# Other places for gate groups, weight loads, query rests and MoBA values in a hybrid attention layer on one Trainium2 core

## The chip, the cores and the metric

The kernel runs on one core of a Trainium2 chip. The core has TensorE (PE, with its weight loads shown as PEld), VectorE (DVE), ScalarE (ACT), GpSimd (POOL) and SyncE (SP), which here issues nearly all DMAs. The metric is the device time of one execution in microseconds. Three executions of the kernel before gave 666.95, 663.0 and 665.05 us, a median of 665.05.

## The reference

One layer is computed for a prompt of 512 tokens and for 8 samples with one new token and 1024 cached positions each; both share all weights. Two token mixers run on the same modulated input, are projected up, merged by sigmoid gates, projected out and normalized. Cut to what matters:

```python
shift, scale, gate = jnp.split(jax.nn.silu(c) @ w_ada + b_ada, 3, axis=-1)
h = x * (1.0 + scale[:, None, :]) + shift[:, None, :]
parts = jnp.split(h @ w_in, np.cumsum(IN_WIDTHS)[:-1], axis=-1)
(a_q, a_kc, a_vc, a_ks, a_vs, a_kw, a_vw, a_g, a_z, b_q, b_k, b_v, b_z, m_a, m_b) = parts
...
o_a = nsa_attention(...)    # compressed blocks + selected blocks + window, gated per head
o_b = moba_attention(...)   # top-3 past blocks by q . mean(k), and the own block
y_a = (o_a.reshape(bsz, t, NSA_WIDTH) * jax.nn.silu(a_z)) @ w_up_a
y_b = (o_b.reshape(bsz, t, MOBA_WIDTH) * jax.nn.silu(b_z)) @ w_up_b
mixed = (jax.nn.sigmoid(m_a) * y_a + jax.nn.sigmoid(m_b) * y_b) @ w_out
x_new = layer_norm(DEEPNORM_ALPHA * x + gate[:, None, :] * mixed, ln_g, ln_b)
```

The cached keys and values of the samples come from paged pools in HBM. The third part of `w_ada`, which gives `gate`, is 1024 x 1024.

## The kernel before

**Columns of work.** The kernel multiplies the 520 columns of tokens (512 + 8) by blocks of 128 weight columns. One such block is a *dense*: 48 matmuls in the order of instructions (24 for each half of the tokens), with the tokens and the weights each split into a high and a low fp32r part (hTh, hTl; hl holds both parts of a weight). Names of denses: q and z (queries and gate path of the sparse mixer), bq, bk, bv, bz (MoBA), ma and mb (the two merge gates; "m6" is ma6 and mb6). The table FILLS says which denses fill which stage. The result of a merge gate that is ready before the last stage is written to `m_d` in HBM and read again later.

**Stages.** 0 to 57 us: the modulation, with its weights ada_ss. 57 to 160: the compression network on cached pages (`phis`), merged with FILLS[0]. 160 to 177: compressed branch. 177 to about 491: eight `attend(pi)`, one for each pair of heads of the prompt, each merged with a part of the samples' attention (`dec`, from cached pages) and with the denses of FILLS[1..8]. About 491 to 549: the denses of FILLS[9], the gate groups g0 to g3 and the rest of `dec`. From 549: `up`, out projection, norm.

**What sets the order.** A `Flow` wraps a generator that yields its costs; `merge` always steps the flow with the smallest share done, so the yields, DEC_SHARE, DEC, DEC_PACE, PHIS and ATT set the order of PE's instructions. From the first pair to the end of FILLS[9], `behind` chains PE's instructions and `queue` chains SP's loads in the order in which the code issues them; SP's queue holds a load until its buffer is free, and all that stands behind it waits too. At most eight of SP's DMAs are under way.

**Weights.** W is a feed with four raw buffers (NRAW; tile raw, 128x1024, 0.52 MB) and three split buffers (hl). `use` (L320) serves a dense and asks for weights two ahead; `take` serves a gate group with raw tiles of ada_g and asks up to three ahead. ACT writes the high part (L305), DVE or GpSimd the low part (L226). A gate group (gen_gate, tile s) is eight matmuls of 512 columns in the trace.

**Pages.** The samples' pages come through C with two buffers (CRAW): slck (selected keys), wink, mobk, slcv (selected values, gathered by an indirect DMA that GpSimd issues), winv, and mobv, the MoBA values, sixteen blocks of four loads of 0.26 MB.

**Inside a pair.** `prepare` splits the queries of a pair into high parts (ACT) and rests, for head groups g = 0 and 1: DVE makes the rest in q2 (L1000), GpSimd that in qx (L1002). `probs` ends with GpSimd's scaling of p (L1051), which the transposes in `turn` (L191, pt) read.

Of the kernel before, what the change touches and what calls it, by code (L numbers as in the profile page):

```python
# [18 lines left out]
T = 512  # L19
# [18 lines left out]
         ["m2", "m3"],  # L38
         ["z0", "bv1", "m4"],
         ["z1", "m5"],  # L40
         ["bk1", "bv2", "z2"],
         ["bk2", "bv3", "bk3"],
         ["z3", "bz0"],
         ["bz1", "m6"],
         ["bz2", "g0", "g1", "bz3", "g2", "g3", "m7"]]
CMP_FILLS = ["bq3", "bk0", "bv0"]
DEC_SHARE = [0.1, 0.236, 0.375, 0.51, 0.575, 0.63, 0.765, 0.89]
DEC, DEC_PACE = 58800.0, 0.9
PHIS = 49353.58399999998
ATT = [16000] * 4 + [8000] * 3 + [10400]  # L50
SECOND = [3, 4, 6, 7]
LIM = 0, 384, 384, 768
# [6 lines left out]
LO_ENG = "dp", "pd", "dp"  # L59

SEQ = (COLS[:3]
       + [n for f in (FILLS[0], CMP_FILLS, *FILLS[1:]) for i in f if i != "ks" for n in ([f"ma{i[1]}", f"mb{i[1]}"] if i[0] == "m" else
                                          [f"g{2 * int(i[1])}", f"g{2 * int(i[1]) + 1}"] if i[0] == "g" else [i])]
       + [n for c in range(8) for n in [f"up{c}"] + ([f"wo{c // 2 - 1}"] if c % 2 and c > 1 else [])]
       + ["wo3"])
# [64 lines left out]
def f32(ap):  # L130
    return ap.bitcast(F32)
# [32 lines left out]
def build(tc, A):  # L164
    nc = tc.nc
# [52 lines left out]
    D = {}  # L218
# [12 lines left out]
    with ExitStack() as es:  # L231
# [35 lines left out]
        class Feed:  # L267
# [49 lines left out]

            def use(self):
                u = self.used = self.used + 1
                self.load_to(self.units[u][0] + 2)  # L320
                self.split_to(u + 1)
                return self.part.pop(u)

# [246 lines left out]
        DENSE = 16 * 333  # L570
# [79 lines left out]
        TM = {}  # L650
# [8 lines left out]
                return pair(tag, dtype)  # L659
            return D["fm"].tile([128, 2, NT], dtype, name="m", tag="m", bufs=7)  # L660

        def gen_m(c):

            if "fm" in D:
                t = TM[c] = m_tile(F32, TM_TAGS[c])
            for i, n in enumerate(("ma", "mb")):
                acc = yield from dense(f"{n}{c}")
                to = t[:, i] if "fm" in D else D["at"].tile([128, NT], F32, name="mg", bufs=2)
                for bk in range(2):
                    nc.scalar.activation(to[:, HALF[bk]], acc[bk][:, :HB], AF.Tanh, scale=0.5)  # L670
                if "fm" not in D:
                    post(lambda to=to, i=i: ld(m_d[c][:, i], to))
                    D["put"] = c + 1
# [16 lines left out]
                nc.scalar.copy(D["ga"][hf], p)  # L690

        def fill_cost(names):
            return max(1.0, sum(2 * DENSE if n[0] == "m" else 1000 if n[0] == "g" else 1700 if n == "ag" else 1 if n == "ks" else DENSE for n in names))

        def fills(names):
            for n in names:
                k = int(n[-1]) if n[-1].isdigit() else 0
                if n == "ks":
                    yield from gen_k(n, ksn[:, 0, :], first["ks"])
                elif n == "kw":  # L700
                    yield from gen_k(n, ksn[:, 1, :])
                elif n in ("vs", "vw"):
                    yield from gen_v(n, 0 if n == "vs" else 1)
                elif n == "ag":
                    yield from gen_gates()
                elif n[0] == "q":
                    yield from gen_q(n, k)
                elif n[0] == "m":
                    yield from gen_m(k)
                elif n[0] == "g":  # L710
                    yield from gen_gate(k)
                elif n[0] == "z":
                    yield from gen_z(n, k)
                elif n[:2] == "bq":
                    yield from gen_q(n, 4 + k)
                elif n[:2] == "bz":
                    yield from gen_z(n, 4 + k)
                elif n[:2] == "bv":
                    yield from gen_v(n, 2 + k)
                else:  # L720
                    yield from gen_k(n, ksm[:, k, :])
# [72 lines left out]
        def phi_prompt(kc, vc):  # L794
            ut = []
            for kv, ev in enumerate((kc, vc)):
                u = u_tile()
                ut.append(u[:, :, 0:528].rearrange("p x (l n) -> p x l n", l=8))
                with tc.issue_after(D["act"].ins), tc.issue_after(D["dve"].ins):
                    nc.scalar.copy(ut[kv][:, 0, :, 64:66], pos[:, kv])  # L800
                    nc.vector.tensor_sub(ut[kv][:, 1, :, 64:66], pos[:, kv], f32(ut[kv][:, 0, :, 64:66]))
                eh = pp.tile([128, 2, 512], F32R, name="eh", tag="craw", bufs=2)
                nc.scalar.copy(eh[:, 0], ev[:, :T])
                lo(eh[:, 1], ev[:, :T], eh[:, 0])
                for x, cp in enumerate((nc.scalar.copy, nc.vector.tensor_copy)):
                    v = f32(eh[:, x]).rearrange("p (u l s) -> p l u s", l=8, s=2)
                    for g in range(2):
                        for l2 in range(2):
                            cp(ut[kv][OWN[l2], x, :, g * 32:g * 32 + 32], v[OWN[g], :, :, l2])
            yield 3000  # L810
            gl = yield from units(64, lambda kv, x, l: ut[kv][:, x, l, :])
            p = p_pt()
            for j, (wa, x) in enumerate(((w2h, 0), (w2l, 0), (w2h, 1))):
                mm(p[:, 0:64], wa[:, 0:128], gl[:, x, :64], j == 0, j == 2)
            for j, (x, wa) in enumerate(((0, w2h), (0, w2l), (1, w2h))):
                mm(p[:64, 64:128], gl[:, x, :64], wa[:, 128:192], j == 0, j == 2)
            yield 600
            x2 = pp.tile([128, 64], F32, name="x2")
            nc.scalar.activation(x2, p[:, 0:64], AF.Identity, scale=0.5, bias=phib[:, 1:2])
            nc.scalar.copy(ck2[:, 0, :], x2)  # L820
            lo(ck2[:, 1, :], x2, ck2[:, 0, :], "d")
            for g in range(2):
                rows = slice(g * 32, g * 32 + 32)
                nc.vector.scalar_tensor_tensor(cv2[rows, g], p[rows, 64:128], 0.5, b2v[rows], op0=OP.mult, op1=OP.add)
# [12 lines left out]
        def phi_pair(bp):  # L837

            us = [u_tile().rearrange("p x (k q u) -> p x q k u", k=16, q=16) for _ in range(2)]
            for ch in range(4):  # L840
                load_chunks(bp * 4 + ch + 1)
                raw = craw.pop(bp * 4 + ch)
                for kv in range(2):
# [1 line left out]
                    dh, dl = (us[kv][:, x, ch * 4:ch * 4 + 4] for x in range(2))  # L845
                    nc.scalar.copy(dh, src)  # L846
                    lo(dl, src, dh)
                yield 0
            uv = [u.rearrange("p x q k u -> p x (k q u)") for u in us]
            gl = yield from units(256, lambda kv, x, l: uv[kv][:, x, l * 256:l * 256 + 256])  # L850
            p = p_pt()
# [133 lines left out]
        def prepare(pi):  # L985
# [8 lines left out]
            for g in range(2):  # L994
                own, oth = OWN[g], OWN[1 - g]

                q2 = at.tile([128, T], F32R, name="q2", bufs=3)
                qx = at.tile([128, T], F32R, name="qx", bufs=3)
                nc.scalar.copy(q2[own], y[own, pi, :T])  # L999
                nc.vector.tensor_sub(q2[oth], y[own, pi, :T], f32(q2[own]))  # L1000
                nc.scalar.copy(qx[oth], y[own, pi, :T])
                nc.gpsimd.tensor_sub(qx[own], y[own, pi, :T], f32(q2[own]))  # L1002
                Q2[pi, g] = q2, qx

        GRP = [[(0, 0), (0, 1), (0, 2), (0, 3)], [(1, 1), (1, 2), (1, 3), (3, 3)], [(2, 2), (2, 3)]]
# [204 lines left out]
        def new_p(d):  # L1210
# [2 lines left out]
            tr(p[:8, :128], d, ident)  # L1213
            t = de.tile([8, 128], F32, name="np", bufs=2)
            nc.vector.tensor_copy(t, p[:8, :128])
            yield 600
            return t

        def own_p(x, col, name):
# [4 lines left out]
        def dec_a():  # L1224
# [23 lines left out]
                yield from C.fetch(0 if q else 1000)  # L1248
            nc.vector.tensor_add(xw[:, :512], xw[:, :512], s)
            nc.vector.tensor_copy(xw[:, 512:513], snew[:, 1:2])  # L1250
            nc.vector.tensor_add(xs[:, 896:1024], xs[:, 896:1024], bdn[:, 0:128])
            late = nc.vector.tensor_copy(xs[:, 1024:1025], snew[:, 0:1])
            xv = xs[:, 64:960].rearrange("p (j c) -> p j c", j=14)
            nc.vector.tensor_add(xv, xv, dn[:, :14, None].to_broadcast([128, 14, 64]))
            softmax(xs, 1025, gd[:, 1:2], de)
# [50 lines left out]
        def dec_b():  # L1306
# [8 lines left out]

            xo = D["xo"]
            nc.vector.tensor_mul(xo, xo, mask("maskn").rearrange("p (a c) -> p a c", a=3))
            yield 500
            total()
            yield 700  # L1320
            p = p_e()
            for i in range(3):
                mm(p[:, :32], xo[:, i], const("seln"), i == 0, i == 2)
# [10 lines left out]
            nc.vector.tensor_add(xv, xv, dm[:, :4, None].to_broadcast([128, 4, 256]))  # L1334
            softmax(xm, 1025, ones, de)
            dm2 = own_p(xm, 1024, "onem")
            yield 1500
            tpm = yield from turn_p([xm[:, k * 128:k * 128 + 128] for k in range(8)], True)
            nm = yield from new_p(dm2)
            p = p_e()  # L1340
# [1 line left out]
                mm(p[grp(t), :128], nm[:, grp(t)], vnew[:, 2 + t], True, True)  # L1342
            xn = de.tile([128, 128], F32, name="xn")
            nc.vector.tensor_mul(xn, p[:, :128], mask("maskh"))
            yield 300
            om = {}
            for q in range(2):
                o = p_e()
# [5 lines left out]
                    yield from C.fetch(1000)  # L1354
                x = om[q] = de.tile([128, 512], F32, name="xo2", tag="x" if q else "xw")
                nc.vector.tensor_mul(x, o, mask("maskm"))
            yield 300
            p = D["ym"] = p_e()
            mm(p[:, :32], xn, const("selx"), True, False)
            for q in range(2):  # L1360
# [16 lines left out]
                yield fa.done - d  # L1377

        done = 0.0
        for pi in range(8):  # L1380
            fl = Flow(fills(FILLS[pi + 1]), fill_cost(FILLS[pi + 1]))
            if pi == 0:

                for _ in range(8):
                    fl.step()
                fl.total, fl.done = fl.total - fl.done, 0.0
            merge(Flow(attend(pi), ATT[pi]), Flow(part(DEC_SHARE[pi]), max(1.0, (DEC_SHARE[pi] - done) * DEC)), fl)
            done = DEC_SHARE[pi]
        while posts:
            posts.pop(0)()  # L1390
# [5 lines left out]
        ga = D["ga"] = [fm.tile([128, 512], F32, name="ga", bufs=2) for _ in range(2)]  # L1396
        for c in range(D.get("put", 0)):
            TM[c] = m_tile(F32, TM_TAGS[c])
            ld(TM[c], m_d[c])
        merge(Flow(fills(FILLS[9]), fill_cost(FILLS[9])), Flow(part(2.0), max(1.0, (1 - done) * DEC / DEC_PACE)))  # L1400
        while posts:
            posts.pop(0)()
        behind[0] = queue[0] = False
# [217 lines left out]
                lo(t[:, 1], src, t[:, 0])  # L1621

        for c in range(8):
            up(c)
            if c == 1:
                spread_gate()
# [151 lines left out]
```

## Time and profile before

| what | us |
|---|---|
| median of three executions | 665.05 |
| the profiled execution, its own time | 666.75 |
| its span in the trace | 665.0 |
| PE busy | 605.9 |
| DVE / ACT / POOL busy | 320.0 / 296.0 / 288.2 |
| bytes moved by DMA | 124.80 MB, 188 GB/s on average |
| mean granted clock of TensorE | 0.963 |

The page gives for each engine its busy time, then the span in 40 slices of 16.6 us, the chain of work that ended last, the costliest groups, and the DMA issues with their landing times. In a timeline the bracket behind an instruction says how long its engine was idle before it and what ended that.

### The profile page before, as it was taken

The page shows a single profiled execution, that of the slowest core. Times are in us where ns is not written, and L with a number is a line of the kernel's source. Part 1 is how long each engine was busy: PE and PEld are TensorE (multiplying, and loading weights), DVE is VectorE, ACT ScalarE, POOL GpSimd, SP SyncE. Part 2 cuts the span into 40 slices and gives each one's busy share as a digit, 9 for nine tenths or more (in the row PEclk, how much of TensorE's full clock was granted, in tenths as well). Part 3 has the DMA queues.
Part 4 walks back from the last instruction along what each step waited for, and adds up shares of the span by engine and source line. Part 5 has one row for each costly group of instructions (what it writes and reads, how often), then busy time and mean ns, then how long its engine had stood idle before and what let it go on. Part 6 is the DMA issues. An engine that isn't in the chain of part 4 may idle for free.

```text
span 665.0 us, 13243 instructions
## 1 busy us (share of the span) xinstructions
PE 605.9 (91%) x4709; PEld 504.1 (76%) x4709; DVE 320.0 (48%) x817; ACT 296.0 (45%) x678; POOL 288.2 (43%) x327
## 2 busy tenths in 40 slices
PE   5999999999889999999996899989992699999993
PEld 3787899999868878776774789867671379999673
DVE  3455344443854665634642447664310127556167
ACT  3365365534545656455451556554420134433521
POOL 2042765532534434433452544444300128655646
PEclk9998999999989999999996999999996989999997
DMA  8984556521356663767971755417789744345203
GB/s 313 405 304 135 174 150 184 145 79 49 99 164 179 203 218 127 253 220 254 286 246 58 289 189 190 143 60 262 240 291 407 261 163 145 107 131 181 73 13 117
DMA packets 63956, 124.80 MB, mean 188 GB/s; under 512 B 8402, under 2 KB 26642, under 8 KB 63378
## 3 DMA queue, kind: packets, MB, share of 16 engines
q1 hardware_dynamic: 62482, 119.76, 53.8%
q0 software_dynamic: 1408, 4.20, 1.8%
q8 instruction: 37, 0.61, 0.4%
q14 instruction: 29, 0.24, 0.1%
HBM read 114.34 MB, written 9.58 MB: 186 GB/s over the span
## 4 chain that ended last, share of the span: by engine, by line
PE 66%; DMA 14%; DVE 5%; ACT 4%; SPq 4%; issue 4%; POOL 2%; POOLq 0%; ACTq 0%; DVEq 0%
PE d L172 37%; PE s L172 9%; PE e L172 7%; PE pt L191 4%; DMA raw<-w_cols 4%; SPq L199 3%; PE o L175 3%; PE o L172 3%; DMA craw<-cmp 2%; DMA raw<-mobv 2%; DMA raw<-ada_g 2%; DMA y<-ada_ss 1%; DMA xr<-xT 1%; PE pt L172 1%; PE e L175 1%
## 5 line engine op out<-in xcount | busy, mean ns | idle before, releaser
L172 PE MATMUL d<-hTh,hl 128*128 128x260 f32 (+1 forms) x1408 | 277.9, 293 | 1.7 <-DVE v L603 1.7
L172 PEld LDWEIGHTS d<-hTh,hl 128*128 128x128 f32 (+1 forms) x1408 | 219.5, 189 | 26.7 <-issue 18.1
L172 PE MATMUL d<-hTl,hl 128*128 128x260 f32 (+1 forms) x704 | 200.6, 285 | 0.0
L172 PEld LDWEIGHTS d<-hTl,hl 128*128 128x128 f32 (+1 forms) x704 | 132.6, 188 | 0.5
L305 ACT CAST hl<-raw 128x512 fp32r<-128x512 f32 (+1 forms) x111 | 67.9, 615 | 85.4 <-PE d L172 51.5
L226 POOL TENSOR_TENSOR hl<-raw,hl 128x512 fp32r<-128x512 f32 x55 | 72.7, 1322 | 64.1 <-ACT hl L305 43.2
L1049 ACT ACTIVATE p<-s,sm 128x512 f32<-128x512 f32 (+1 forms) x96 | 50.6, 527 | 69.9 <-DVE sm L1046 59.9
L226 DVE TENSOR_TENSOR hl<-raw,hl 128x512 fp32r<-128x512 f32 (+1 forms) x56 | 52.8, 944 | 59.2 <-ACT hl L305 59.0
L1051 POOL TENSOR_SCALAR p<-p,sm,gp 128x512 f32<-128x512 f32 (+1 forms) x64 | 40.4, 633 | 94.0 <-DVE sm L1050 88.3
L172 PE MATMUL d<-yh,hl 128*128 128x260 f32 x256 | 46.5, 283 | 0.0
L191 PE MATMUL pt<-cst,p 128*128 128x128 f32 x240 | 39.6, 280 | 5.4 <-POOL p L1051 5.1
L1046 DVE CUSTOM_DVE_ANT_0 s<-s,band 128x256 f32<-128x256 f32 (+1 forms) x48 | 17.4, 363 | 48.7 <-PE s L172 45.8
L172 PEld LDWEIGHTS d<-yh,hl 128*128 128x128 f32 x256 | 39.7, 188 | 1.3 <-issue 0.4
L191 PEld LDWEIGHTS pt<-cst,p 128*128 128x128 f32 x240 | 27.6, 142 | 16.7 <-POOL p L1051 8.0
L1051 POOL TENSOR_SCALAR p<-p,sm,cst 128x512 f32<-128x512 f32 (+3 forms) x32 | 19.6, 612 | 45.3 <-DVE sm L1050 43.5
L172 PE MATMUL d<-yl,hl 128*128 128x260 f32 x128 | 35.8, 283 | 0.0
L172 PE MATMUL s<-u,w1h 128*128 128x256 f32 (+1 forms) x160 | 30.8, 286 | 5.0 <-ACT u L846 2.7
L172 PE MATMUL s<-kd,q 128*128 128x512 f32 (+1 forms) x96 | 32.4, 338 | 0.0
L226 POOL TENSOR_TENSOR u<-craw,u 128x512 fp32r<-128x512 f32 x16 | 21.8, 1369 | 24.1 <-ACT u L846 24.0
L172 PE MATMUL s<-kd,qx 128*128 128x512 f32 (+1 forms) x96 | 31.0, 323 | 0.0
L175 PE MATMUL o<-pp,v 128*64 128x384 f32 (+3 forms) x168 | 30.6, 437 | 0.0
L1002 POOL TENSOR_TENSOR qx<-y,q 64x512 fp32r<-64x512 f32 x16 | 24.2, 1512 | 14.6 <-ACT q L999 9.5
(414 smaller groups left out, 1139.7 us busy)
## 6 DMA issues: line engine op xcount, KB each, us to landing
raw<-w_cols SPq DMA_DIRECT2D x46, 512.0 KB, 5.3
raw<-mobk SPq DMA_DIRECT2D x64, 256.0 KB, 4.2
raw<-mobv SPq DMA_DIRECT2D x64, 256.0 KB, 4.1
craw<-cmp SPq DMA_DIRECT2D x64, 128.0 KB, 2.2
u<-ada_ss SPq DMA_DIRECT2D x12, 512.0 KB, 8.9
raw<-slck SPq DMA_DIRECT2D x64, 64.0 KB, 2.1
raw<-ada_g SPq DMA_DIRECT2D x8, 512.0 KB, 6.8
raw<-w_up SPq DMA_DIRECT2D x8, 512.0 KB, 3.8
```

What stands on the lines that cost most here:

```text
L172: i = mmraw(out, lhsT, rhs, start=start, stop=stop, skip_group_check=True)
L175: i = mmraw(out, lhsT, rhs, start=start, stop=stop, skip_group_check=True)
L191: return in_turn(nc.tensor.transpose(out, x, unit))
L199: i = nc.sync.dma_start(out, x)
L226: (nc.gpsimd if eng == "p" else nc.vector).tensor_sub(out, x, f32(hi))
L305: nc.scalar.copy(h, src)
L1002: nc.gpsimd.tensor_sub(qx[own], y[own, pi, :T], f32(q2[own]))
L1046: nc.vector.tensor_tensor_reduce(out=s[:, b:n], in0=s[:, b:n], in1=j.band[:, 256 - (n - b):], scale=1.0, scalar=top, op0=OP.add, op1=OP.mi ...
L1049: nc.scalar.activation(pr, s[:, :n], AF.Exp, scale=-1.0, bias=sm[:, 1:2], accum_out=sm[:, 2:3])
L1051: D.setdefault("pool", []).append(nc.gpsimd.tensor_scalar(pr, pr, sm[:, 3:4], j.gate(i), op0=OP.mult, op1=OP.mult))
```

## The change

The kernel after is built from the same functions. FILLS[5] to FILLS[9] are dealt out anew, so that the gate groups stand apart with denses between them; `gen_m` can make half a merge gate for that (ma6 in one pair, mb6 in the next). `use` asks for weights three ahead while the queue is chained. The two rests of head group 0 both go to GpSimd, those of group 1 to DVE. Of the m_d reloads only two are issued at the start of the last stage, the others in the `up` loop (where the scheduler moves three of them forward again). The shares, costs and yields of the decode flow are set anew, so that the first MoBA value blocks are fetched one pair sooner, and the compression stage gets larger yields.

```diff
-         ["bk1", "bv2", "z2"],
-         ["bk2", "bv3", "bk3"],
-         ["z3", "bz0"],
-         ["bz1", "m6"],
-         ["bz2", "g0", "g1", "bz3", "g2", "g3", "m7"]]
+         ["bk1", "bv2", "bk2", "bv3"],
+         ["bk3", "z2", "z3"],
+         ["bz0", "ma6"],
+         ["bz1", "mb6"],
+         ["g0", "bz2", "g1", "bz3", "g2", "m7", "g3"]]
-DEC_SHARE = [0.1, 0.236, 0.375, 0.51, 0.575, 0.63, 0.765, 0.89]
-DEC, DEC_PACE = 58800.0, 0.9
-PHIS = 49353.58399999998
+DEC_SHARE = [0.1, 0.235, 0.38, 0.525, 0.595, 0.69, 0.805, 0.92]
+DEC, DEC_PACE = 61350.0, 0.95
+PHIS = 64350.0
...
                 u = self.used = self.used + 1
-                self.load_to(self.units[u][0] + 2)
+                self.load_to(self.units[u][0] + (3 if queue[0] else 2))
...
-        def gen_m(c):
+        def gen_m(n):
+            c = int(n[-1])
...
-            for i, n in enumerate(("ma", "mb")):
-                acc = yield from dense(f"{n}{c}")
+            for i in ([0, 1] if len(n) == 2 else ["ab".index(n[1])]):
+                acc = yield from dense(f"m{'ab'[i]}{c}")
...
-            yield 3000
+            yield 7000
...
-                yield 0
+                yield 500
...
-                nc.vector.tensor_sub(q2[oth], y[own, pi, :T], f32(q2[own]))
+                eng = (nc.gpsimd, nc.vector)[g]
+                eng.tensor_sub(q2[oth], y[own, pi, :T], f32(q2[own]))
                 nc.scalar.copy(qx[oth], y[own, pi, :T])
-                nc.gpsimd.tensor_sub(qx[own], y[own, pi, :T], f32(q2[own]))
+                eng.tensor_sub(qx[own], y[own, pi, :T], f32(q2[own]))
...
-            yield 1500
+            yield 2400
             tpm = yield from turn_p([xm[:, k * 128:k * 128 + 128] for k in range(8)], True)
...
+        def dec_flow(until, pace=1.0):
+            f = Flow(part(until), max(1.0, (min(until, 1.0) - done) * DEC / pace))
+            f.done = max(0.0, fa.done - done * DEC)
+            return f
+
         for pi in range(8):
             fl = Flow(fills(FILLS[pi + 1]), fill_cost(FILLS[pi + 1]))
-            if pi == 0:
-                for _ in range(8):
+            if pi in (0, 5):
+                for _ in range(9 if pi else 8):
                     fl.step()
                 fl.total, fl.done = fl.total - fl.done, 0.0
-            merge(Flow(attend(pi), ATT[pi]), Flow(part(DEC_SHARE[pi]), max(1.0, (DEC_SHARE[pi] - done) * DEC)), fl)
+            merge(Flow(attend(pi), ATT[pi]), dec_flow(DEC_SHARE[pi]), fl)
...
         for c in range(D.get("put", 0)):
             TM[c] = m_tile(F32, TM_TAGS[c])
+        for c in range(2):
             ld(TM[c], m_d[c])
-        merge(Flow(fills(FILLS[9]), fill_cost(FILLS[9])), Flow(part(2.0), max(1.0, (1 - done) * DEC / DEC_PACE)))
+        merge(Flow(fills(FILLS[9]), fill_cost(FILLS[9])), dec_flow(2.0, DEC_PACE))
...
         for c in range(8):
+            if 2 <= c + 2 < D["put"]:
+                ld(TM[c + 2], m_d[c + 2])
             up(c)
```

**How the order moves.** PE in the last stage before, where the first two gate groups stand (s is the gates' sum, raw with a number one raw tile, d a dense, e the samples' MoBA values):

```order
L172 MATMUL d_6670<-hTh_73,hl_6673 128x260 x2
L172 MATMUL d_6670<-hTl_74,hl_6673 128x260
L172 MATMUL s_6767<-raw_6671,cs_75 32x512
L175 MATMUL s_6767<-raw_6671,cs_75 32x512
L175 MATMUL s_6767<-raw_6506,cs_75 32x512 x2
L172 MATMUL s_6767<-raw_6770,cs_75 32x512
L175 MATMUL s_6767<-raw_6770,cs_75 32x512
L175 MATMUL s_6767<-raw_6768,cs_75 32x512 x2
L172 MATMUL e_6528<-raw_6686,tp_5916 32x512
```

The same engine after the change, at its second gate group:

```order
L172 MATMUL d_6709<-hTh_73,hl_6715 128x260 x2
L172 MATMUL d_6709<-hTl_74,hl_6715 128x260
L172 MATMUL s_6699<-raw_6702,cs_75 32x512
L175 MATMUL s_6699<-raw_6702,cs_75 32x512
L175 MATMUL s_6699<-raw_6700,cs_75 32x512 x2
L172 MATMUL e_6459<-raw_6650,tp_5917 32x512
L175 MATMUL e_6459<-raw_6650,tp_5917 32x512 x3
L172 MATMUL d_6818<-hTh_73,hl_6822 128x260 x2
```

The two groups of a pair, four raw tiles in a row, are now parted by a whole dense and a value block.

SP's queue before, in the last stage between two runs of MoBA value loads:

```order
L199 DMA raw<-mobv 128x512
L199 DMA raw<-ada_g 128x1024 x2
L199 DMA raw<-w_cols 128x1024
L199 DMA raw<-ada_g 128x1024 x2
L731 TENSOR_LOAD ptt
```

The queue after the change, where the last stage begins (kd and v are buffers that take a reloaded m_d):

```order
L199 DMA raw<-mobv 128x512
L199 DMA m_d<-mg 128x520
L199 DMA kd<-m_d 128x1040 x2
L199 DMA raw<-ada_g 128x1024 x2
L199 DMA raw<-w_cols 128x1024
L199 DMA kd<-m_d 128x1040
L199 DMA v_6694<-m_d 128x1040
L732 TENSOR_LOAD ptt
```

Seven reloads ahead of everything have become two ahead and two behind the first gate tiles and a weight.

GpSimd before, at the gather of selected values (p is a probability tile, gp the mixer's gate):

```order
L1163 DMA raw<-slcv,vidx 128x1024 x2
L1051 TENSOR_SCALAR p<-p,sm,gp 128x512
L1051 TENSOR_SCALAR p<-p,sm,gp 128x384
L1163 DMA raw<-slcv,vidx 128x1024 x2
L1051 TENSOR_SCALAR p<-p,sm,gp 128x256
L1002 TENSOR_TENSOR qx<-y,q_4560 64x512
L1051 TENSOR_SCALAR p<-p,sm,gp 128x128
```

GpSimd after, at the same gathers:

```order
L1165 DMA raw<-slcv,vidx 128x1024 x2
L1053 TENSOR_SCALAR p<-p,sm,gp 128x128
L226 TENSOR_TENSOR hl<-raw,hl 128x512
L1165 DMA raw<-slcv,vidx 128x1024 x2
L1053 TENSOR_SCALAR p<-p,sm,gp 128x512
L1053 TENSOR_SCALAR p<-p,sm,gp 128x384
L1053 TENSOR_SCALAR p<-p,sm,gp 128x256
L1053 TENSOR_SCALAR p<-p,sm,gp 128x128
L1165 DMA raw<-slcv,vidx 128x1024 x2
```

No rest of the queries stands behind the first four gathers now.

More of the change, by code (lines that the diff above doesn't have):

```diff
@@ L61 @@
 SEQ = (COLS[:3]
-       + [n for f in (FILLS[0], CMP_FILLS, *FILLS[1:]) for i in f if i != "ks" for n in ([f"ma{i[1]}", f"mb{i[1]}"] if i[0] == "m" else
+       + [n for f in (FILLS[0], CMP_FILLS, *FILLS[1:]) for i in f if i != "ks" for n in ([f"ma{i[1]}", f"mb{i[1]}"] if i[0] == "m" and len(i) == 2 else
                                           [f"g{2 * int(i[1])}", f"g{2 * int(i[1]) + 1}"] if i[0] == "g" else [i])]
@@ L692, in fill_cost @@
         def fill_cost(names):
-            return max(1.0, sum(2 * DENSE if n[0] == "m" else 1000 if n[0] == "g" else 1700 if n == "ag" else 1 if n == "ks" else DENSE for n in names))
+            return max(1.0, sum((4 - len(n)) * DENSE if n[0] == "m" else 1000 if n[0] == "g" else 1700 if n == "ag" else 1 if n == "ks" else DENSE for n in names))
         def fills(names):
@@ L708, in fills @@
                 elif n[0] == "m":
-                    yield from gen_m(k)
+                    yield from gen_m(n)
                 elif n[0] == "g":
@@ L1215, in new_p @@
             nc.vector.tensor_copy(t, p[:8, :128])
-            yield 600
+            yield 700
             return t
@@ L1250, in dec_a @@
             nc.vector.tensor_copy(xw[:, 512:513], snew[:, 1:2])
-            nc.vector.tensor_add(xs[:, 896:1024], xs[:, 896:1024], bdn[:, 0:128])
-            late = nc.vector.tensor_copy(xs[:, 1024:1025], snew[:, 0:1])
+            late = nc.vector.tensor_add(xs[:, 896:1024], xs[:, 896:1024], bdn[:, 0:128])
+            nc.vector.tensor_copy(xs[:, 1024:1025], snew[:, 0:1])
             xv = xs[:, 64:960].rearrange("p (j c) -> p j c", j=14)
@@ L1317, in dec_b @@
             nc.vector.tensor_mul(xo, xo, mask("maskn").rearrange("p (a c) -> p a c", a=3))
-            yield 500
+            yield 800
             total()
-            yield 700
+            yield 1100
             p = p_e()
@@ L1344, in dec_b @@
             nc.vector.tensor_mul(xn, p[:, :128], mask("maskh"))
-            yield 300
+            yield 700
             om = {}
@@ L1356, in dec_b @@
                 nc.vector.tensor_mul(x, o, mask("maskm"))
-            yield 300
+            yield 600
             p = D["ym"] = p_e()
```

## The prediction

> **What bounds the kernel now.** I read the page first. PE, the matmul engine, is busy for 605.9 us, so only 59 us of the 665.0 us span can be won by better order. The row of slices and the granted clock below it show where those 59 us lie: mostly in slices 30 and 31 (from 499 to 532 us, at 16.6 us a slice), some in slices 21 and 22 (from 349 us) and around 11 (183 us), and where PE pauses for long the clock falls too.
>
> ```profile
> PE 605.9 (91%) x4709; PEld 504.1 (76%) x4709; DVE 320.0 (48%) x817; ACT 296.0 (45%) x678; POOL 288.2 (43%) x327
> PE   5999999999889999999996899989992699999993
> PEclk9998999999989999999996999999996989999997
> PE 66%; DMA 14%; DVE 5%; ACT 4%; SPq 4%; issue 4%; POOL 2%; POOLq 0%; ACTq 0%; DVEq 0%
> ```
>
> The last line is the chain that ended last: two thirds PE, and DMA as the second. The view of PE's waits names what it waits for (total us, times, longest), and the windows (length, then busy us and count for PE, PEld, DVE, ACT, POOL, then clock, DMA share, GB/s) put it into stages.
>
> ```profile
> PE s L172 <- DMA raw<-ada_g: 18.6, 3, 6.6
> PE pt L191 <- POOL p L1051: 5.1, 1, 5.1
> PE e L172 <- DMA raw<-winv: 2.4, 1, 2.4
> 57.00:160.00 103.00, 99.22 (x830) 96.33 (x830) 40.74 (x75) 48.78 (x109) 54.72 (x59) 1.00 0.44 129
> 160.00:200.00 40.00, 35.58 (x266) 32.49 (x264) 25.84 (x73) 18.20 (x43) 16.09 (x19) 0.91 0.39 121
> 340.00:380.00 40.00, 32.44 (x295) 25.97 (x293) 16.15 (x53) 15.58 (x42) 20.74 (x23) 0.87 0.58 203
> 428.00:446.00 18.00, 15.05 (x121) 12.57 (x119) 14.34 (x43) 9.90 (x27) 8.19 (x9) 1.00 0.21 63
> 493.00:550.00 57.00, 38.37 (x273) 26.06 (x273) 7.31 (x12) 9.59 (x20) 9.04 (x12) 0.82 0.75 275
> 550.00:650.00 100.00, 100.00 (x651) 85.16 (x650) 54.71 (x92) 38.93 (x65) 62.28 (x60) 1.00 0.34 112
> ```
>
> So the stage 493 to 550 holds 57 − 38.4 = 18.6 us of idle time, all of it before three of the four gate groups. From 550 on PE has none.
>
> **Term 1, the gate groups (−16).** PE's timeline (start, length, instruction, idle before and releaser) and SP's queue beside it:
>
> ```profile
> 506.26 1.06 PE L172 MATMUL s<-raw,cs 128*32 128x512 f32 x1 [5.75 <-DMA raw<-ada_g]
> 507.11 1.06 PE L172 MATMUL s<-raw,cs 128*32 128x512 f32 x1
> 514.51 1.06 PE L172 MATMUL s<-raw,cs 128*32 128x512 f32 x1 [6.32 <-DMA raw<-ada_g]
> 524.87 0.62 PE L172 MATMUL s<-raw,cs 128*32 128x512 f32 x1
> 525.32 0.59 PE L172 MATMUL s<-raw,cs 128*32 128x512 f32 x1
> 532.49 1.06 PE L172 MATMUL s<-raw,cs 128*32 128x512 f32 x1 [6.55 <-DMA raw<-ada_g]
> ```
>
> ```profile
> 493.20 1.40 SPq L199 DMA_DIRECT2D kd<-m_d  x3
> 496.71 0.70 SPq L199 DMA_DIRECT2D raw<-ada_g  x1
> 498.58 7.99 SPq L199 DMA_DIRECT2D raw<-mobv  x8
> 506.91 1.08 SPq L199 DMA_DIRECT2D raw<-ada_g  x2
> 517.97 7.28 SPq L199 DMA_DIRECT2D raw<-mobv  x8
> 525.30 0.90 SPq L199 DMA_DIRECT2D raw<-ada_g  x2
> ```
>
> A gate is two rounds of matmuls on two tiles of 0.52 MB. Gates come in pairs, the four raw buffers hold the tiles of one gate and of its neighbours, and the second gate's tiles are asked for only when PE reaches the first (506.91 against 506.26, 525.30 against 524.87). Their landing is the stall. After it the rounds step by 0.85 us (506.26 to 507.11), where a warm pair steps by 0.45 (524.87 to 525.32): about nine rounds (two, three and four, the value blocks' rounds right behind the gates among them) at 0.4 more are 3.6 us. Idle and slow clock together: 22.2 us.
>
> The change puts 24 matmuls or more (a dense column block) between gates and asks a tile three ahead. Gate 0's tiles are then asked for during the last pairs and have landed. What is new is a race between queue and PE. Up to the weights of the last dense block, SP's new order holds four reloads of m_d (0.53 MB each), four tiles of ada_g, eight of mobv (0.26) and three of w_cols: 7.9 MB, where the old order had 13 MB (seven reloads, seven, sixteen and three) ahead of w_up. The fastest window shows what that takes:
>
> ```profile
> 500.00:510.00 10.00, 2.44 (x13) 0.50 (x11) 0.42 (x1) 0.39 (x1) 1.41 (x2) 0.68 1.03 405
> raw<-ada_g SPq DMA_DIRECT2D x8, 512.0 KB, 6.8
> ```
>
> At 405 GB/s 7.9 MB last 19.6 us, and PE comes to that block some 18 to 19 us into the stage: two dense blocks of 48 matmuls (at 99.2 / 830 = 0.12 us each, by the compression stage's row, nearly all dense work) are 11.5, three gates and three value blocks of two rounds at 0.45 are 5.4, and waits come on top. A cast is still to do. I take 3 us of new wait there (0 to 6), 1.5 for slack at gate 2 (0 to 3, its tiles land in 6.8 us by the second row) and 1.5 of slow clock behind both (0 to 3). 22.2 − 6 = 16 gained (10 to 22). The Trainium skill, "DMA: Bandwidth & Descriptors", in its table of figures at the top, gives about 358 GB/s as the HBM limit per core. By it the 7.9 MB would take 22.2 us and the sum would be 2.6 us worse; the row of 405 GB/s speaks against it, so the sum goes by the row.
>
> **Term 2, the gather of selected values (−8).** POOL's timeline, then PE's:
>
> ```profile
> 347.38 0.94 POOL L1163 DMA_INDIRECT raw<-slcv,vidx  x1 [0.31 <-issue]
> 353.50 1.26 POOL L1002 TENSOR_TENSOR qx<-y,q 64x512 fp32r<-64x512 f32 x1 [4.23 <-DMA raw<-slcv,vidx]
> 355.37 1.12 PE L191 MATMUL pt<-cst,p 128*128 128x128 f32 x4 [5.13 <-POOL p L1051]
> raw<-slcv,vidx POOLq DMA_INDIRECT x4, 5.9
> 371.89 0.30 PE L172 MATMUL e<-raw,tp 128*32 128x128 f32 x1 [2.42 <-DMA raw<-winv]
> ```
>
> The rest for head group 1 stands on GpSimd behind a wait for all four gathers; p's scaling stands behind the rest, and PE's transposes behind p. In the changed order that rest is VectorE's, and GpSimd waits for gathers only ahead of later gathers. What is late next is PE's own matmul on the gathered values: second issue about 1.9 us after the keys' last matmul, 5.9 us to land (fourth row), against some 5.8 us of PE work between: about 2 us (0 to 4). The winv wait has dense rows worth some 9 us before it in the new order, against a wait of 2.4 now, and goes. Slow clock: 32.4 us of PE at 0.87 bounds it at 4.2; I take 2.5. So 5.1 + 2.4 + 2.5 − 2 = 8 (4 to 11.7).
>
> **Term 3, a weight behind the selected keys (−4).**
>
> ```profile
> 175.42 12.88 SPq L199 DMA_DIRECT2D raw<-slck  x20
> 188.40 0.38 SPq L199 DMA_DIRECT2D raw<-w_cols  x1
> 193.87 1.06 PE L191 MATMUL pt<-cst,c 128*64 128x128 f32 x4 [2.52 <-ACT pp L1060]
> ```
>
> The weight is asked for behind 20 page loads; ACT waits for it in its cast, the eviction pp behind the cast, and PE for pp. Three ahead, that weight stands before the pages. 2.5 us of wait go, and of the clock's share (35.6 us at 0.91 bound it at 3.2) I take 1.5 (total 2.5 to 5.7).
>
> **Smaller terms.** The decode softmax chain leaves 18 − 15 = 3 us idle at 428 to 446. Longer yields put more PE rows between its steps: −2 (−3 to 0). The compression stage 57 to 160 idles 3.8 us, and its new yields let fills in between: −1 (−3.8 to +3, since the same yields can part a chain that had been tight). MoBA values: the sixteen blocks of four loads keep their number, but twelve in place of ten now fall in pairs 6 and 7.
>
> ```profile
> 444.63 15.53 SPq L199 DMA_DIRECT2D raw<-mobv  x16
> raw<-mobv SPq DMA_DIRECT2D x32, 256.0 KB, 3.5
> ```
>
> Four issues take 3.9 us of queue at worst (15.53 / 4), and landing 3.5. With two buffers a block must come back within some 7 us on average, at the tightest places 5.3. One reload of m_d is now issued among them; at 405 GB/s its 0.53 MB add 1.3 us to one block, and the release it waits for (a values' matmul of pair 4 to 6) comes before that block's own. Together +1 (0 to 2.5). The up stage begins with casts of y:
>
> ```profile
> 548.76 3.79 ACT L1416 CAST yh<-y 128x520 fp32r<-128x520 f32 x7 [0.70 <-PE e L172]
> 549.47 3.03 POOL L226 TENSOR_TENSOR yl<-y,yh 128x520 fp32r<-128x520 f32 x2 [2.78 <-ACT yh L1416]
> ```
>
> They hide behind 24 dense matmuls now (2.9 us at 0.12); in the new order only gate 3 stands there, some 0.9 us: +1.5 (0 to 3). The two late reloads of m_d (1.1 MB) fall in a stage whose DMA share is 0.34 and cost nothing; without that cover they would take 2.6 us at 405 GB/s.
>
> **The rests (+2).** Each engine keeps its count, but for head group 0 GpSimd now does two in a row:
>
> ```profile
> L1002 POOL TENSOR_TENSOR qx<-y,q 64x512 fp32r<-64x512 f32 x16 | 24.2, 1512 | 14.6 <-ACT q L999 9.5
> ```
>
> That is 1.5 us more between two p scalings, once in each of eight pairs, hidden while PE has dense blocks in hand. Bounds: −2 (both of group 1 leave GpSimd) to 8 x 1.5 = 12. The one stall behind p in the wait view says that a cover is mostly there, so I take +2.
>
> **Sum.** −16 − 8 − 4 − 2 − 1 + 1 + 1.5 + 2 = −26.5. Against the profiled execution's 666.75 us that is 640.25; it lies 1.7 above the median of 665.05, which is within the runs' own spread. I say **640**. All ends at their best give 618, all at their worst about 671.
>
> **Rivals.**
> - *The waits change hands* (0.17): queue-paced waits return at the gates, the last weights and the gather. Terms 1 and 2 keep their lower ends, 10 and 4, in place of 24: 650, up to 656 with the rests at half their bound. For it: DMA was 0.75 busy in that stage. Against: 5 MB less in it.
> - *Deeper gain* (0.12): no new waits at all; 22 and 10 in place of 24: 632, down to 626.
> - *The third-ahead load does nothing* (0.06): a ring of four raw buffers is full with three ahead, so a load may wait for the same release as before, and SP's queue, which is strictly in order, holds the rest behind it. Then gates wait as before and the result is 662 to 668. Against: gate 0's loads stand a whole pair earlier.
> - *Slower* (0.05): with the queue in order, weights fetched earlier stand ahead of page loads, and each MoBA block comes back late. With two buffers the blocks' spacing is (turnaround + 1 us of use) / 2. It costs from 7 us on, and eats the whole gain when sixteen blocks each lose 26.5 / 16 = 1.7 us beyond their 4.0: a turnaround of 10.4 us. At 11 the time is 672. Against: 3.9 + 3.5 = 7.4 us is the measured sum, at a busy queue.
>
> **How the numbers follow.** Forecast (634 to 648) 0.60, and the four rivals as given. A measurement of this kernel can tell about 0.5%, 3.3 us, from no change. Faster: 0.60 + 0.17 + 0.12 = 0.89; same 0.06; slower 0.05. The range 627 to 657 reaches over the forecast and most of the first two rivals and leaves out the last two.
>
> **What would show it.** Right: the ada_g total among PE's waits falls from 18.6 to under 6, the stage from the seventh reload's place to the first up matmul lasts some 35 to 40 us instead of 55, POOL p no longer releases a long PE wait, the clock row loses its dip in slice 21 and one of those in slices 30 and 32. Wrong: new rows of raw<-mobv, raw<-w_cols or slcv with over 5 us, or PE's busy time itself growing.

## The result, and the profile after

The kernel after takes 643.98 us (median of four, 640.25 to 648.84) against 665.5 us before: a ratio of 0.9685 (95% interval 0.9606 to 0.9763), 21.5 us less. The profiled execution took 648.84 us, the longest of the four, with a span of 647.1 us. Two later runs of the same kernel beside the one before gave 0.9669 (0.9602 to 0.9736) and 0.9682 (0.9629 to 0.9734), with profiled spans of 640.9 and 643.1 us. Of the eleven executions of the kernel before that ran beside the last of these, three that took over 1.5% more than the fastest are left out, which gives it 666.54 us there.

The page of the kernel after: PE's busy time, the slices and the granted clock.

```profile
span 647.1 us, 13237 instructions
PE 599.3 (93%) x4709; PEld 503.3 (78%) x4709; DVE 324.2 (50%) x816; ACT 296.1 (46%) x678; POOL 285.3 (44%) x328
PE   5998999999889989999999999999897899999992
PEclk9999999999999989999999999999999899999997
```

The same 4709 matmuls take 6.6 us less of PE's time (599.3 against 605.9), and idle time falls from 59.1 to 47.8 us. The deep clock dips of slices 21 and 30 are gone, but a shallower one stands in slice 31. These lines of the view of PE's waits say what remains:

```profile
PE pt L191 <- ACT pp L1062: 3.5, 3, 2.0
PE d L191 <- ACT ev L576: 3.5, 2, 2.4
PE s L172 <- DMA raw<-ada_g: 3.1, 1, 3.1
PE d L172 <- POOL hl L226: 2.9, 2, 2.5
PE e L172 <- DMA raw<-mobv: 2.5, 4, 0.8
PE pt L191 <- DVE pp L1062: 2.1, 2, 1.4
PE d L172 <- POOL yl L226: 1.4, 2, 0.9
PE pt L191 <- POOL p L1053: 0.9, 1, 0.9
PE e L172 <- DMA raw<-slcv,vidx: 0.7, 1, 0.7
```

The gate tiles' 18.6 us have become 3.1, and the wait for winv is off the list. POOL's p fell from 5.1 to 0.9, and the 0.9 stand at 478.73 us, far from the gathers. New are waits for the casts' low parts (POOL hl); the value loads (mobv) and evictions by DVE (pp) had 0.2 us each and now have over 2. ACT ev, 0.2 before, stands in the modulation and the compression stage, at 52.59 and 71.55 us.

Windows cut at the program's own marks (first score of pair 0, first instruction behind the last pair, first up matmul) compare the two halves of the gain. The kernel before, pairs and last stage:

```profile
177.00:491.40 314.40, 298.58 (x2393) 237.29 (x2391) 165.03 (x514) 156.98 (x406) 128.63 (x157) 0.97 0.61 200
491.40:551.50 60.10, 41.47 (x298) 29.03 (x297) 8.81 (x13) 12.08 (x25) 10.54 (x13) 0.83 0.74 272
```

The kernel after, the same two:

```profile
175.30:486.20 310.90, 296.89 (x2416) 236.44 (x2417) 165.35 (x515) 157.06 (x407) 128.85 (x158) 0.99 0.64 209
486.20:531.30 45.10, 38.94 (x276) 30.04 (x274) 6.75 (x11) 10.73 (x22) 10.11 (x13) 0.89 0.71 258
```

The last stage lost 15.0 us, of which idle time is 18.6 − 6.2 = 12.4. The other 2.5 us are work that moved: the last stage has 22 matmuls less (298 against 276, two value blocks and six matmuls of a dense), and the pairs have them now. At the full-speed steps of the timelines, 0.45 us a round and 0.12 us a matmul of a dense, that is 1.8 + 0.7 = 2.5 us. The pairs lost 3.5 us with this work added, so 6.0 on equal work; their idle time fell from 15.8 to 14.0. In the two later profiles the pairs took 306.2 and 308.7 us and the last stage 43.4 and 43.3. The pairs' gain is thus 3.5 to 8.2 us (6.0 to 10.7 on equal work), and the last stage's 15 to 17 (12.5 to 14.3 on equal work).

### The profile page after: what moved, and what is told of

The parts are those of the page before. It is cut to its first block, busy times and chain, and to the rows that moved or that the text cites. A ratio compares the mean times of both kernels' runs of the same rounds, so it can differ in the third digit from the quotient of the medians.

```text
span 647.1 us, 13237 instructions
## 1 busy us (share of the span) xinstructions
PE 599.3 (93%) x4709; PEld 503.3 (78%) x4709; DVE 324.2 (50%) x816; ACT 296.1 (46%) x678; POOL 285.3 (44%) x328
## 4 chain that ended last, share of the span: by engine, by line
PE 60%; DMA 18%; DVE 8%; ACT 4%; SPq 4%; POOL 3%; issue 3%; POOLq 0%; ACTq 0%; DVEq 0%
PE d L172 34%; PE s L172 9%; PE e L172 6%; DMA raw<-w_cols 5%; PE pt L191 4%; SPq L199 3%; DMA raw<-mobv 3%; PE o L172 2%; PE o L175 2%; DMA craw<-cmp 2%; PE pt L172 2%; DMA y<-ada_ss 1%; DMA raw<-ada_g 1%; DMA xr<-xT 1%; DMA band<-band 1%
## 5 line engine op out<-in xcount | busy, mean ns | idle before, releaser
L226 DVE TENSOR_TENSOR hl<-raw,hl 128x512 fp32r<-128x512 f32 (+1 forms) x56 | 59.2, 1056 | 45.5 <-ACT hl L305 44.4
L1053 POOL TENSOR_SCALAR p<-p,sm,gp 128x512 f32<-128x512 f32 (+1 forms) x64 | 41.8, 653 | 90.1 <-DVE sm L1052 80.4
L1052 DVE RECIPROCAL sm<-sm 128x1 f32<-128x1 f32 x96 | 15.3, 160 | 33.6 <-ACT p L1051 33.2
L1062 ACT COPY pp<-pt 128x512 f32<-128x512 f32 (+1 forms) x48 | 23.0, 479 | 14.6 <-PE pt L191 14.5
```

Source lines behind the costliest of these rows:

```text
L226: (nc.gpsimd if eng == "p" else nc.vector).tensor_sub(out, x, f32(hi))
L1052: nc.vector.reciprocal(sm[:, 3:4], sm[:, 2:3])
L1053: D.setdefault("pool", []).append(nc.gpsimd.tensor_scalar(pr, pr, sm[:, 3:4], j.gate(i), op0=OP.mult, op1=OP.mult))
L1062: j.copied[gi] = (nc.scalar.copy if COPY_ENG[gi] == "a" else nc.vector.tensor_copy)(t[:, :n], p[:, :n])
```

## The experiments

All times are medians. The runs went out in three groups of four, each on one chip beside the kernel before. The change again, the gates paired, two ahead and the rests taken back ran beside 667.69 us; the table alone, the seven reloads, the five late reloads and the rests alone beside 667.74; the other four beside 666.54.

**The change again.** Unedited.

> The changed kernel as it is, for a second profile and more times beside it. Its first profiled execution (648.84 us) was the longest of four (640.25 to 648.84). If the difference lies in waits of a few us that come and go with DMA landings, the second profile shows the same places (gate 1's tiles, the casts' low part POOL hl, MoBA values) with other lengths; a time of 640 to 649 again. If the first profile was a disturbed one, 640 to 643 and shorter waits.

645.13 us (642.66 to 646.66), profiled 642.66. The same places wait with other lengths: gate 1's tiles 1.8 us, casts of weights (ACT hl and POOL hl) 4.5, mobv 1.8. The first profile was the upper end of the kernel's own spread.

**Gates paired again, everything else kept.**

```diff
-         ["g0", "bz2", "g1", "bz3", "g2", "m7", "g3"]]
+         ["bz2", "g0", "g1", "bz3", "g2", "g3", "m7"]]
```

> The changed kernel with the last stage's table in the old order (bz2, g0, g1, bz3, g2, g3, m7): same blocks, gates in pairs again. Theory (parting the gates is what removed the waits, since the second gate's tiles are asked for only at the first): two waits of 5 to 7 us return before the second gates of the pairs, with slow clock behind them, 10 to 15 us slower than the changed kernel, 653 to 659. Rival (the queue was freed by moving the reloads and fetching a tile further ahead, and the parting is idle): under 3 us slower.

650.86 us, 5.7 more than the changed kernel beside it (645.13): between theory and rival. PE's timeline of this kernel, second gates of the two pairs:

```profile
496.62 1.06 PE L172 MATMUL s<-raw,cs 128*32 128x512 f32 x1 [6.80 <-DMA raw<-ada_g]
...
510.92 0.62 PE L172 MATMUL s<-raw,cs 128*32 128x512 f32 x1 [2.05 <-DMA raw<-ada_g]
...
511.37 0.96 PE L172 MATMUL s<-raw,cs 128*32 128x512 f32 x1
```

The first pair waits as the theory said. The second waits only 2.05 us: with the third tile its second gate's loads go out at 502.36, 5.4 us ahead of the first gate's own matmuls at 507.80. The parting is worth some 6 us on top of the rest.

**The table alone, on the kernel before.**

```diff
-         ["bz2", "g0", "g1", "bz3", "g2", "g3", "m7"]]
+         ["g0", "bz2", "g1", "bz3", "g2", "m7", "g3"]]
```

> The kernel before with only the last stage's table in the new order. Theory: parting alone removes the waits of two of the three gates, but seven reloads still stand ahead of gate 1's tiles: one long wait of 6 to 10 us stays, the sum of waits for ada_g falls from 18.6 to 8 or so, 9 to 13 us faster than before (652 to 656). Rival (the parting does nothing without the reloads moved): within 3 us of before.

674.46 us, **slower** than before by about 1%: ratio 1.0118 (1.0055 to 1.0180). Both expectations missed. No gate waits any more, but the denses do. Its waits, SP's queue and PE's timeline:

```profile
PE d L172 <- ACT hl L305: 21.0, 3, 12.7
```

```profile
492.13 1.40 SPq L199 DMA_DIRECT2D kd<-m_d  x3
...
495.70 0.52 SPq L199 DMA_DIRECT2D raw<-w_cols  x1
...
515.30 0.42 SPq L199 DMA_DIRECT2D raw<-w_cols  x1
...
531.84 0.90 SPq L199 DMA_DIRECT2D raw<-w_cols  x2
```

```profile
505.83 0.58 PE L172 MATMUL d<-hTh,hl 128*128 128x260 f32 x1 [12.68 <-ACT hl L305]
...
521.29 0.59 PE L172 MATMUL d<-hTh,hl 128*128 128x260 f32 x1 [3.49 <-ACT hl L305]
...
537.94 0.38 PE L172 MATMUL d<-hTh,hl 128*128 128x260 f32 x1 [4.83 <-ACT hl L305]
```

With weights two ahead, each dense behind a gate has its weight asked for only about when that gate is served, behind seven reloads the first time (495.70, used 505.83). The wait changed its name from the gate's tile to the dense's weight, and grew.

**The table and the third tile, on the kernel before.** The edit above, and:

```diff
-                self.load_to(self.units[u][0] + 2)
+                self.load_to(self.units[u][0] + (3 if queue[0] else 2))
```

> The kernel before with the last stage's new table and weights three ahead, nothing else. The table alone made it slower (674.46), with 21 us of waits for the cast of weights in place of 18.6 for gate tiles. Theory (with two ahead the dense behind a gate asks for its weight too late, and the third tile repairs that): the waits behind ACT hl fall from 21 to under 9, 8 to 15 us faster than the table alone, 659 to 666. Rival (the bytes ahead, seven reloads and sixteen value loads, set the stage): waits only change their name again, 669 or more.

660.37 us, 14 less than the table alone had on another chip and 6 less than before (0.9895, 0.9825 to 0.9965). The waits behind ACT hl fall to 0.4 us; one gate waits 6.2 us behind seven reloads, and casts 3.5 us on POOL:

```profile
PE s L172 <- DMA raw<-ada_g: 6.2, 1, 6.2
PE d L172 <- POOL hl L226: 3.5, 2, 2.7
```

The theory holds: with the kernel before as it was, the parting pays only with the third tile.

**Two ahead, everything else kept.**

```diff
-                self.load_to(self.units[u][0] + (3 if queue[0] else 2))
+                self.load_to(self.units[u][0] + 2)
```

> The changed kernel with weights two ahead everywhere. Theory (the third tile is what puts a weight before the selected keys and gate 0's tiles a step earlier): the wait of about 2.5 us near 190 us returns with its slow clock, some wait at the gates, 3 to 7 us slower. Rival (the raw ring is full with three, and the load waits for the same release): within 1.5 us.

651.3 us, 6.2 more than the changed kernel beside it. The size is as expected, the place is not: near 190 us no wait for a weight returned (PE waits 0.81 there for pp, as in the changed kernel), and the loss stands behind gate 0 in PE's timeline:

```profile
481.91 0.59 PE L172 MATMUL s<-raw,cs 128*32 128x512 f32 x1
...
491.98 0.58 PE L172 MATMUL d<-hTh,hl 128*128 128x260 f32 x1 [9.46 <-ACT hl L305]
```

**All seven reloads at the start of the last stage.**

```diff
-        for c in range(2):
+        for c in range(D.get("put", 0)):
             ld(TM[c], m_d[c])
...
-            if 2 <= c + 2 < D["put"]:
-                ld(TM[c + 2], m_d[c + 2])
```

> The changed kernel with all seven reloads of m_d at the start of the last stage again. Theory (bytes ahead in the queue set when gate 1's tiles land): five more reloads, 2.7 MB, stand before gate 1's tiles, 6 to 7 us at 405 GB/s; the wait of 3.05 us there grows to 7 to 10, with slow clock, 5 to 9 us slower than the changed kernel. Rival (reloads are hidden, only the parting counts): within 2 us.

648.31 us at 0.9723 (0.9680 to 0.9765), some 3 us above the changed kernel's 645 on the other chips, less than expected. Gate 1's tiles now come late:

```profile
498.59 1.06 PE L172 MATMUL s<-raw,cs 128*32 128x512 f32 x1 [8.03 <-DMA raw<-ada_g]
```

The wait grew to 8.0 us as the theory said; the whole paid less than the wait, since the casts' waits behind it (2.3 us in place of 4.5) shrank.

**Five reloads behind the last gate's tiles.** The opposite edit, in the chained queue:

```diff
-        for c in range(2):
-            ld(TM[c], m_d[c])
         merge(Flow(fills(FILLS[9]), fill_cost(FILLS[9])), dec_flow(2.0, DEC_PACE))
         while posts:
             posts.pop(0)()
+        for c in range(5):
+            ld(TM[c], m_d[c])
         behind[0] = queue[0] = False
...
-            if 2 <= c + 2 < D["put"]:
+            if 5 <= c + 2 < D["put"]:
```

> The changed kernel with five of the reloads issued behind the last gate's tiles and three w_up loads, in the chained queue, none ahead of a gate's tiles or among the MoBA values. If gate 1's wait of 3.05 us is made by the bytes ahead of its tiles, the tiles land 2 to 3 us earlier and the wait falls below 1 us, and the later weights gain too: 2 to 5 us faster than the changed kernel. Against it: the first up block needs its reload at once, and if the queue holds it behind a w_up load that waits for its buffer, up to 3 us come back there.

640.71 us (640.37 to 641.31), ratio 0.9591 (0.9562 to 0.9620), and 7.6 us less than with all seven reloads first, on the same chip. No gate waits:

```profile
483.22 0.87 SPq L199 DMA_DIRECT2D raw<-ada_g  x2
...
517.83 1.37 SPq L199 DMA_DIRECT2D kd<-m_d  x3
```

```profile
482.60 0.62 PE L172 MATMUL s<-raw,cs 128*32 128x512 f32 x1
...
490.74 0.62 PE L172 MATMUL s<-raw,cs 128*32 128x512 f32 x1
```

Gate 1's tiles are asked for at 483.22 with no reload before them, and gate 1 runs at 490.74 without a wait.

> The kernel with the five late reloads once more, beside the changed kernel on one chip. If the gain is real: median 2 to 6 us under the changed kernel and a narrower spread, since no gate tile waits; if the first times were a matter of the chip: within 1.5 us.

> The changed kernel, unedited, beside the one with late reloads on the same chip: 642 to 647, with a wait of 1.5 to 3 us for the second gate's tiles.

On one chip: 640.73 us (638.69 to 644.26, six runs) against 645.15 us (643.38 to 647.26, six runs) for the changed kernel, whose gate 1 waited 2.1 us and whose casts waited 4.9. Four of the six times lie below all six of the changed kernel, so a gain of about 4.4 us holds; the narrower spread of the first run was not seen again. This version beats both kernels.

**The rests taken back, everything else kept.**

```diff
-                eng = (nc.gpsimd, nc.vector)[g]
-                eng.tensor_sub(q2[oth], y[own, pi, :T], f32(q2[own]))
+                nc.vector.tensor_sub(q2[oth], y[own, pi, :T], f32(q2[own]))
                 nc.scalar.copy(qx[oth], y[own, pi, :T])
-                eng.tensor_sub(qx[own], y[own, pi, :T], f32(q2[own]))
+                nc.gpsimd.tensor_sub(qx[own], y[own, pi, :T], f32(q2[own]))
```

> The changed kernel with one rest on each engine again for both head groups. Theory (the rest of group 1 behind GpSimd's gathers made the stall): GpSimd's rest waits for four gathers again, PE waits 4 to 6 us behind p, 5 to 8 us slower than the changed kernel. Rival (the new pacing of the samples' flow parted gathers and rests): no wait over 1 us there, within 2 us. If instead the doubled rests on GpSimd cost something elsewhere, it is faster.

645.32 us, the same as the changed kernel (645.13): the theory missed, the rival holds. GpSimd's rest still stands behind the gathers and starts 5.7 us after the last of them is issued, hardly sooner than before (6.1). But two scalings of p stand between in place of one, so GpSimd idles 1.84 us in place of 4.23, which the view puts down to an eviction. PE works on the gathered values first, and its next transposes of p wait for nothing:

```profile
344.94 0.95 POOL L1164 DMA_INDIRECT raw<-slcv,vidx  x1 [0.30 <-issue]
...
350.62 1.39 POOL L1003 TENSOR_TENSOR qx<-y,q 64x512 fp32r<-64x512 f32 x1 [1.84 <-ACT pp L1061]
...
354.81 0.60 PE L191 MATMUL pt<-cst,p 128*128 128x128 f32 x4
```

**The rests alone, on the kernel before** (that edit the other way round).

> The kernel before with only the rests dealt by head group. Theory: the stall of 5.1 us behind p near 355 us goes, PE waits 1 to 3 us at the gathered values in its place, and slow clock goes too: 3 to 7 us faster than before. Rival (the stall only moves to the gathered values, which land at the same time): PE waits 4 us or more for slcv, within 2 us of before.

660.34 us, 7.4 less than before (0.9868, 0.9829 to 0.9908). POOL's p falls from 5.1 to 0.7 in the waits, winv keeps 2.0, and no wait for the gathered values takes their place:

```profile
PE pt L191 <- POOL p L1052: 0.7, 1, 0.7
```

The gain is larger in the pairs than in the whole. They took 303.6 us here against 314.3 in the kernel before, with the same work, while the start up to the first score, which the edit does not touch, took 183.1 against 177.1. The wait near 190 us also shrank, from 2.5 to 0.86, with weights two ahead and the old pacing.

**Rests and pacing taken back.** The rests as above, and DEC_SHARE, DEC, DEC_PACE, the yields of the samples' flow and its carried-over progress as before. The change had also swapped two VectorE instructions of the samples' scores; their order went back too.

> The changed kernel with the old rests and the old shares, costs and yields of the samples' flow. Putting only the rests back cost nothing. Theory (two cures for one stall: the new pacing parts gathers and rest by time, the new rests by engine): with both taken back PE waits 3 to 6 us behind p, or behind the rest, at the gathers again. One MoBA block also falls back into the last stage, so the whole is 6 to 14 us slower than the changed kernel, of which the gather's place shows 4 to 8. Rival (the blocks dealt anew or the third tile parted them): no wait over 1.5 us at the gathers.

653.78 us, 8.6 more than the changed kernel. The stall is back, on POOL and PE:

```profile
350.58 1.26 POOL L1003 TENSOR_TENSOR qx<-y,q 64x512 fp32r<-64x512 f32 x1 [4.05 <-DMA raw<-slcv,vidx]
352.45 1.12 PE L191 MATMUL pt<-cst,p 128*128 128x128 f32 x4 [4.95 <-POOL p L1052]
369.01 0.30 PE L172 MATMUL e<-raw,tp 128*32 128x128 f32 x1 [2.23 <-DMA raw<-winv]
...
507.33 0.62 PE L172 MATMUL e<-raw,tp 128*32 128x512 f32 x1 [3.64 <-DMA raw<-mobv]
```

So the stall at the gathers had two cures in this change, and either is enough: the rests on another engine, or a pacing that puts more work between gathers and rest. The waits for winv and for snew (1.2 us) came back with the old pacing too, and a value block in the last stage waited 3.6 us, so the stall at the gathers is only a part of the 8.6.

No run takes apart the new deal of FILLS[5] to FILLS[8], the yields of the compression stage, or the parts of the new pacing.

## Why the prediction was right, point by point

The forecast was 640 us, in the range 627 to 657; the measured 643.98 lies 4 us above the forecast. The direction and the largest term came from the right view: three waits for gate tiles in a stage of 38 us of work. That the number came so close is in part luck, as the lengths of the stages in the profiles (us) show:

| profile | up to the first score | pairs | last stage | from the first up matmul |
|---|---|---|---|---|
| before | 177.1 | 314.3 | 60.1 | 113.5 |
| after | 175.3 | 310.9 | 45.1 | 115.8 |
| after, second | 175.7 | 306.3 | 43.4 | 115.5 |
| after, third | 174.0 | 308.7 | 43.3 | 117.1 |

The two large terms came out smaller than forecast, and the start gained more than the 1 us that it was given.

**Term 1 (−16): the mechanism right, the size somewhat large.** The last stage is 15 to 17 us shorter, but 2.5 of that is work moved into the pairs, so the term itself measured 12.5 to 14.3, within its range of 10 to 22. The new waits that I put at 4.5 us measured 6.2 in the first profile: 3.05 at gate 1 and 3.1 at casts and low parts of weights. I had given gate 1 none, and gate 2 and the last dense all. Slow clock, of which I let 1.5 us remain, cost about as much as before in the first profile: on equal work PE was busy 38.9 us in this stage before and after. In the two later profiles it was 1.9 and 2.7 us less. One reading was also too simple: the wait of 5.75 us stood before the first gate of a pair, so the pairing did not make it; one of that gate's tiles went out only at 496.71, behind the seven reloads.

```profile
497.43 0.62 PE L172 MATMUL s<-raw,cs 128*32 128x512 f32 x1 [3.05 <-DMA raw<-ada_g]
514.12 0.39 PE L172 MATMUL d<-hTh,hl 128*128 128x260 f32 x1 [2.54 <-POOL hl L226]
486.20:497.40 11.20, 8.18 (x66) 6.16 (x64) 0.85 (x2) 1.37 (x3) 1.42 (x2) 1.00 1.00 372
```

The last row is the window from gate 0 to gate 1: at a DMA share of 1.00 the engines moved 372 GB/s, not the 405 that the sum used. The Trainium skill's figure of about 358 GB/s ("DMA: Bandwidth & Descriptors", the table at its top) was nearer for this stretch than the row I preferred; the measured 372 lies above it. What the prediction did not separate, the runs did: the parting alone costs 7 us, the third tile turns that into a gain of 6, and the reloads' place decides 3 to 4 us to each side.

**Term 2 (−8): right for the kernel, wrong as a lone cause.** Idle time at the gathers and at winv went as said, the wait left at the gathered values was 0.7 us in place of 2, and the granted clock of 340 to 380 us rose from 0.87 to 1.00. But the sentence that put it on VectorE's taking over the rest is only half: the new pacing alone does it (rests taken back, no change in time).

**Term 3 (−4): the mechanism as said, too much credit.** The third tile does put a weight before the pages: two weights are issued at 163.49, ahead of the pages at 172.99, where before one was. But it is not needed for it: with two ahead the weight is issued behind twenty pages as before (186.04) and its cast at 190.83 waits for nothing. In that kernel ACT comes to the cast 15.0 us after the pair's first score, in the kernel before 13.0 us after it. The rests alone, with neither edit, left 0.86 us of this wait, so here too there was more than one cure. 2.5 us of wait became 0.8, and 0.8 for DVE's pp came next to it, so idle time fell by 1.1 us and not by 2.5. The clock's part came out larger than my 1.5 us, up to its bound of 3.2: the granted clock of 160 to 200 us rose from 0.91 to 1.00 in two profiles of three, 0.96 in the other.

**The pairs as a whole: mis-sized.** Terms 2 and 3, the softmax chain and the additions for MoBA values and rests gave −11; the profiles gave −3.5 to −8.2, or −6.0 to −10.7 on equal work. The removed waits are gone, but waits of 0.5 to 2 us took their place, where I had counted 1 for values and 2 for rests: mobv 2.5, DVE's pp 2.1 (one of them behind a load of masks that stands in SP's queue), 0.7 for np, and in one profile 2.0 for ACT's pp at 235 us. The doubled rests on GpSimd cost nothing that can be measured, so the +2 was for the wrong engine. In the first profile this is a shortfall of 5 us against the sum, in the second almost none. The rests alone had shortened the pairs of the kernel before by 10.7 us in their profile (by 8.4 against the pairs of the table alone, 312.0 us), about as much as the whole change at its best, so no further gain of the other edits shows in the pairs.

**Smaller terms.** The start was 1.4 to 3.1 us shorter up to the first score (−1 said) than in the one profile of the kernel before. But the three other profiles with the old start took 178.4, 183.0 and 183.1 us up to there, and all ten with the new one 174.0 to 176.0, so its gain was probably larger, about 5 us by the means. What made it stays open. The up stage took 2.0 to 3.6 us more (+1.5 said), 0.6 to 1.4 us of it for POOL's low part of y.

**The rivals.** Waits did change hands in part; that case lay at 650 (its upper end of 656 should have been 654, since the sum already holds 2 us for the rests). The third-ahead load was not idle: without it the changed kernel loses 6.2 us. The slower case, value loads coming back late, cost 2.5 us in four waits. A slower outcome was near by another road, which I had not listed: the same table without the third tile.

## What to carry to other kernels

Parting two users of a prefetched ring moves the wait to whoever stands behind them, unless the fetch distance grows with it: look at what the next unit asks for, and when, before counting the wait as gone. In a queue that is strictly in order, loads that are needed late belong behind those needed now; here five reloads (2.7 MB), moved behind the last gate's tiles, gave another 4.4 us. When a change has several edits, take back one at a time and then two: an edit that costs nothing to take back may be one of two cures for the same stall. And before a stage is called faster, count whether its work moved elsewhere.

## What the runs showed of the hardware

The granted clock can fall after waits of only 2 to 3 us, and with a delay. After the wait of 2.05 us with the gates paired the first round still steps by 0.45 us, and the next lasts 0.96; after the 3.05 us at gate 1 of the changed kernel two rounds ran at full speed (497.43, then 0.59 us at 497.88) before the next took 0.97. After 6.80 us the first round is slow at once (1.06). After a wait of 2.00 us at 235.36 in the same profile as the 3.05, away from the gates, the matmuls of a dense took 0.64 us a pair in place of 0.40. The Trainium skill, "TensorE: Matmul & The Clock Gate", Part 1, gives an idle window of about 3.4 us for the drop; a wait of 2.05 us lies below that, so here the measurement decides that shorter waits can be followed by a drop. They are not always: after 2.11 us at gate 1 in the third profile of the changed kernel, and after 2.33 us at 178.33 in the first, the matmuls that followed kept their full speed.
